# Later first Fourier steps, another order of the matmuls in a weight tile, and fewer background loads: a hybrid diffusion backbone on one core

## The chip, the core and the metric

The kernel runs as one program on one core of a Trainium2 chip. The metric is the device time in microseconds (us) from the start of the program to its end on that core. Times are medians of several runs; the profile comes from one execution, and its figures are set against that execution's own time. The engines named here are PE (TensorE: matmuls; "PEld" is its weight load), DVE (VectorE), ACT (ScalarE), and SP (SyncE, which issues all the loads). Arrays in the on-chip memory have 128 partitions.

## The reference

Two layers over 256 tokens of width 2048, with a context of 256 tokens. The even layer has retention heads, a Fourier mixing and gates; the odd layer is a gated short convolution. Cut to what matters here:

```python
def _fourier(u, fno_w):
    b, L, _ = u.shape
    ug = u.reshape(b, L, G_B, GB_DIM).astype(jnp.float32)
    f = jnp.fft.fft2(ug, axes=(1, 3), norm='ortho').real
    y = jnp.einsum('blgc,gcd->blgd', f.astype(u.dtype), fno_w)
    return y.reshape(b, L, B_WIDTH)
...
def _even_layer(hx, hc, w_in, decay_logit, fno_w, w_out, need_ctx):
...
    yx = jnp.concatenate([_merge_heads(ret_x, hx.dtype) * jax.nn.silu(gax),
                          _fourier(ux, fno_w) * jax.nn.silu(gbx)], axis=-1) @ w_out
...
def _odd_layer(h, w_in, conv_w, w_out, rows):
    bg, cg, xt, g = jnp.split(h @ w_in, 4, axis=-1)
    y = bg * _conv3(cg * xt, conv_w, rows) * jax.nn.silu(g)
    return y @ w_out

def reference(x, c, ctx, c_ctx, ada_w, ada_b, norm_w, ev_w_in, ret_decay_logit, fno_w, ev_w_out,
              od_w_in, conv_w, od_w_out, final_norm_w):
...
    for i in range(DEPTH):
        shift_x, scale_x, gate_x = jnp.split((sc @ ada_w[i] + ada_b[i])[:, None, :], 3, axis=-1)
...
        hx = _modulate(x, norm_w[i], shift_x, scale_x)
...
        x = x + gate_x * yx
    return _rmsnorm(x, final_norm_w)
```

All of it is float32. Nearly all the work lies in the products `h @ w_in` and `y @ w_out`, some 400 MB of weights, each read once.

## The kernel before

**A product.** The activations are kept transposed, channels on partitions, and split in two: 256 columns of a rounded high part and 256 of the rest, one after the other (`split_act`, `modulate`). A weight tile is 1 MB, 128 x 2048, loaded by `load_raw` into one of three buffers `raw`. `split_w` cuts it into four pieces of 512 columns; for each, ACT casts the high part `whi` (line 94) and DVE subtracts it to get the low part `wlo` (line 59), six buffers of each. `group_t` (line 126) computes 256 output channels from two or four such tiles: a piece holds two slices of 128 input channels (`k2`), and for each slice and each half `m` of the output channels there are two matmuls, both noted at line 56. The first, called H here, multiplies 128 x 128 of `whi` with all 512 columns; the second, L, multiplies the same part of `wlo` with the first 256. So a tile is 16 pairs of H and L, and a group of two tiles 32 pairs. Sums stay in PSUM; `lr` then adds the two column halves. `group_n` (name `gN`) and `group_d` (`gD`) are variants with three matmuls a step, all of 512 or all of 256 columns.

**Work hung between.** Two lists run beside the groups. `hook()` pops one entry of `stages` after the second and the fourth piece of a tile, so four times in a group of two tiles: a *quarter*. `bg()` pops a background task at the start of a tile: it loads one row block of `adaT` (1 MB, in a `raw` buffer) and reduces it on DVE (line 378) to one column of modulation values. There are 64 tasks. With `quiet[0]` set none is taken, with `often[0]` set one at every tile, without it one at every second. `finish_mods(first, last)` runs the tasks still missing up to `last`, all at once, and then uses their values.

**The order.** (1) Context and first retention pair, until about 154 us. (2) Four pairs of retention heads, until about 527; keys go to two streams (token and context), the rest to one. Background tasks run in it up to the fourth pair's queries. (3) Fourier stage. `u0` and `u1` are the two halves of the folded Fourier input; each takes 16 steps, `step(kc)`, of six matmuls into `pu` and two into `pd`, on weights that `fold(kc)` makes ahead: a sum and a difference on DVE (`ef`, lines 65 and 68), then the same cast and subtraction as above. `step(0)` also runs `fold(0)`. These steps are hung into the groups of the Fourier gate, `gate_of(0..3)` for `u0` and `gate_of(4..7)` for `u1`, one a quarter. Steps 0, 2, 4, 6 of `u0` also fold the activations (`fold_x`). The buffers of this stage, `ef` among them, are taken from a pool that opens when the retention's pool has been closed. (4) The even layer's output projection, `project(w0o)`: eight row blocks of four tiles, of which the first, `t_out`, still carries the last Fourier pieces; `quiet` is off from there to the fifth, and set for the blocks 6 and 7. (5) The odd layer: 16 blocks, each four groups of two tiles; background tasks from its second block on, at every second tile. (6) Its projection, `project(w1o)`, again eight row blocks, and the final norm.

Each engine works through its own queue in order. The order in these queues is made when the program is built: instructions are placed by a simulated timeline, the earlier one in the program first among those that the simulation finds ready. So a matmul may stand ahead of one that is written before it.

Of the kernel before, what the change touches and what calls it, by code (L numbers as in the profile page):

```python
# [22 lines left out]
H = 8  # L23
# [12 lines left out]
def body(tc, a, out):  # L36
    nc = tc.nc
    es = ExitStack()
    with es:
# [6 lines left out]
        def psum(name):  # L46
            return pp.tile([P, 2, 512], F32, tag="ps", name=name)
# [7 lines left out]
        def mm(o, l, r, start, stop):  # L55
            nc.tensor.matmul(o, l, r, start=start, stop=stop, skip_group_check=True)  # L56
# [7 lines left out]
        def add(o, x, y):  # L64
            nc.vector.tensor_tensor(o, x, y, op=ALU.add)  # L65
# [17 lines left out]
        def load_raw(src):  # L83
            raw = wp.tile([P, 2048], F32, tag="raw", name="raw")
            nc.sync.dma_start(raw[:], src)
            return raw
# [10 lines left out]
        def split_w(raw, spare=None):  # L97

            parts = []
            for pc in range(4):  # L100
                w = tuple(t[:] for t in spare()) if spare and pc == 3 else slot()
                cut(raw[:, pc * 512:(pc + 1) * 512], *w)
                parts.append(w)
            return parts

        tasks, stages = [], []

        turn = [0]
        quiet = [False]
        often = [True]  # L110

        def bg():

            if quiet[0]:
                return
            turn[0] ^= 1
            if tasks and (turn[0] or often[0]):
                tasks.pop(0)()

        def hook():  # L120
            if stages:
                f = stages.pop(0)
                if f is not None:
                    f()

        def group_t(wd, i0, nkt, streams):

            ps = [psum("gT") for _ in streams]
            for kt in range(nkt):
                raw = load_raw(wd[i0 + kt])  # L130
                bg()
                for pc, (hi, lo) in enumerate(split_w(raw)):
                    for k2 in range(2):
                        kc = kt * 8 + pc * 2 + k2
                        fst, lst = kc == 0, kc == nkt * 8 - 1
                        for t, st in zip(ps, streams):
                            x = st[kc // 2]
                            for m in range(2):
                                c0 = k2 * 256 + m * 128
                                mm(t[:, m, :], hi[:, c0:c0 + 128], x[:, kc % 2, :], fst, False)  # L140
                                mm(t[:, m, 0:256], lo[:, c0:c0 + 128], x[:, kc % 2, 0:256], False, lst)
                    if pc % 2:
                        hook()
            return ps
# [129 lines left out]
        def gather():  # L274

            gs = rp.tile([P, 512], F32, tag="cst", name="gs")
            nc.vector.tensor_copy(gs[:], gp[:])
            return gs
# [63 lines left out]
        for e in range(8):  # L342
            w = wn
# [14 lines left out]
            if more:  # L358
                gemv(raws[3], 3)
                gs = gather()  # L360
# [115 lines left out]
        for pr in range(4):  # L476
# [23 lines left out]
            def heads():  # L500
                return [retention(hh, mk[hh], q, k, kc, lambda: vbox[0]) for hh in range(2)]

            if pr == 0:
                kc = rp.tile([P, 2, 256], F32, tag="kc", bufs=1, name="kc")
# [3 lines left out]
                h0, h1 = heads()  # L508
                stages += [None, h0[0], h1[0], h0[1], h0[2], h1[1], None, h1[2]]
                keep((pvx, pvc))  # L510
            elif pr < 3:
                k, kc = keys()
                q = queries()
                h0, h1 = heads()
# [3 lines left out]
            else:  # L518
                k, kc = keys()
# [5 lines left out]
                h0, h1 = heads()  # L525
# [8 lines left out]
            for hh, hd in enumerate((h0, h1)):  # L534
                y = yA[2 * pr + hh] = act_tile(YA[2 * pr + hh], f"yA{2 * pr + hh}")
                t = hd[3]["t"]
# [215 lines left out]
        u0, u1 = half(0), half(1)  # L752
        gs = [fourier(g, u0 if g < 4 else u1) for g in range(8)]

        def both(*fs):
            def f():
                for x in fs:
                    x()
            return f

        def folds(kc):
            def f():
                if kc % 2 == 0 and kc < 8:
                    fold_x(fp, 4 + kc // 2)
                    ends(4 + kc // 2)
            return f

        stages += [both(lambda kc=kc: u0.step(kc), folds(kc)) for kc in range(15)]
        stages += [both(lambda: u0.step(15), gs[0][0])]
        for g in range(4):  # L770
            gate_of(g)

# [3 lines left out]
        for g in range(4, 8):  # L776
# [4 lines left out]
        g4[2]()  # L781
        stages += [both(g4[3], g5[1], g6[0], g5[2]), both(g4[4], g5[3], g6[1], g7[0], g6[2]),
                   both(g5[4], g6[3], g7[1], g7[2]), both(g6[4], g7[3]), g7[4]]
        quiet[0] = False
        t_out, = group_t(a["w0o"], 0, 4, [ys])
        f_es.close()

# [11 lines left out]
        def project(wd, xs, gcol, xin, acc, first=None, post=None):  # L799


            def res(b, m, v, src):
                nc.vector.scalar_tensor_tensor(x1[b][:, m, :], v, mods[:, gcol + 2 * b + m:gcol + 2 * b + m + 1],
                                               src[:, m, :], op0=ALU.mult, op1=ALU.add)

            tot = None
            for b in range(8):
                src = xin(b)
                quiet[0] = b >= 6
                if b < 7:  # L810
                    t = first if b == 0 and first is not None else group_t(wd, 4 * b, 4, [xs])[0]
                    s = lr(l1, t)
                    for m in range(2):
                        res(b, m, s[:, m, :], src)
                    if b == 0:
                        nc.scalar.square(acc[:], x1[b][:])
                    else:
                        sq = l1.tile([P, 2, 256], F32, tag="t2", bufs=5, name="sq")
                        nc.scalar.square(sq[:], x1[b][:])
                        add(acc[:], acc[:], sq[:])  # L820
                    for m in range(2 if post is not None else 0):
                        nc.scalar.activation(x1[b][:, m, :], x1[b][:, m, :], AF.Copy,
                                             scale=cols[:, post + 2 * b + m:post + 2 * b + m + 1])
                else:
                    t = group_d(wd, 4 * b, 4, xs)
                    tot = bank("tot")
                    for m in range(2):
                        mm(tot[:, 0:256], ones[:], acc[:, m, :], m == 0, False)

                    warm = l1.tile([P, 1], F32, tag="warm", name="warm")  # L830
                    nc.scalar.activation(warm[:], acc[:, 0, 0:1], AF.Sqrt)
                    sq = l1.tile([P, 2, 256], F32, tag="t2", bufs=5, name="sq")
                    for m in range(2):
                        res(b, m, t[:, m * 256:m * 256 + 256], src)
                        nc.scalar.square(sq[:, m, :], x1[b][:, m, :])
                        mm(tot[:, 0:256], ones[:], sq[:, m, :], False, m == 1)
            return rstd_bc(l1, tot[:, 0:256], D)
# [6 lines left out]
        acc0 = l1.tile([P, 2, 256], F32, tag="acc", name="acc0")  # L844
        rs1 = project(a["w0o"], ys, 0, reload, acc0, t_out)
        finish_mods(16, 48)
        often[0] = False
        nc.vector.scalar_tensor_tensor(mods[:, 16:32], mods[:, 16:32], 1.0, cols[:, C_NW1:C_NW1 + 16],
                                       op0=ALU.add, op1=ALU.mult)

# [1 line left out]
        h1 = [act_tile(HF[e], f"h1_{e}") for e in range(8)]  # L852
# [3 lines left out]
        w1 = a["w1"]  # L856
        y1 = []
        for b in range(16):
            tcg, = group_t(w1, b * 8, 2, [h1])
            scg = lr(l1, tcg, "scg", 2)  # L860
            txt, = group_t(w1, b * 8 + 2, 2, [h1])
            z = lr(l1, txt, "z", 2)
            mul(z[:], z[:], scg[:])
            cv = l1.tile([P, 2, 256], F32, tag="cv", bufs=2, name="cv")
            for m in range(2):
                w = [cols[:, C_CV + j * 32 + 2 * b + m:C_CV + j * 32 + 2 * b + m + 1] for j in range(3)]
                z4 = z[:, m, :].rearrange("p (r w) -> p r w", w=64)
                c4 = cv[:, m, :].rearrange("p (r w) -> p r w", w=64)
                nc.vector.tensor_scalar(cv[:, m, :], z[:, m, :], w[1], None, op0=ALU.mult)
                nc.vector.scalar_tensor_tensor(c4[:, :, 1:64], z4[:, :, 0:63], w[0], c4[:, :, 1:64],  # L870
                                               op0=ALU.mult, op1=ALU.add)
                nc.vector.scalar_tensor_tensor(c4[:, :, 0:63], z4[:, :, 1:64], w[2], c4[:, :, 0:63],
                                               op0=ALU.mult, op1=ALU.add)
            tbg, = group_t(w1, b * 8 + 4, 2, [h1])
            sbg = lr(l1, tbg)
            mul(cv[:], cv[:], sbg[:])
            tg, = group_t(w1, b * 8 + 6, 2, [h1])
            sg = silu_lr(l1, tg, "t2", 5)
            mul(cv[:], cv[:], sg[:])
            y1.append(act_tile(YA[b] if b < 8 else f"hx{b - 8}", f"y1_{b}"))  # L880
            split_act(y1[b], cv[:])
            quiet[0] = False
# [123 lines left out]
```

## Time and profile before

| | |
|---|---|
| median of 3 runs | 1856.43 us (1849.19 to 1857.1) |
| profiled execution, its time | 1855.88 us |
| profiled execution, its span | 1854.1 us |
| mean granted clock of PE | 0.987 |
| read from memory | 397 MB, 215 GB/s over the span |

The profile's page lists the busy time of each engine, then the span in 40 equal slices, the load queues, the chain of work that ended last (followed back from the last instruction, at each step to what released it), and the costliest groups of instructions. A group reads: line, engine, operation, output and inputs by the program's names, shapes, count | busy time in us, mean ns of one | idle time before them and what ended it. Matmuls are pipelined, so the listed length of one is longer than the distance to the next one; distances are read from starts, or from a row of the chain with its length and count.

### The profile page before, as it was taken

The numbers are of one execution on the slowest core, as the hardware profiler recorded it, in microseconds if no ns is written. First come the engines' busy times: TensorE is split into PE (matmuls) and PEld (weight loads), VectorE is DVE, ScalarE is ACT, GpSimd is POOL, SyncE is SP. The second block draws the span as 40 slices with busy tenths as digits, with TensorE's granted clock in tenths as the row PEclk, the third lists the DMA queues.
The fourth block names the chain that finished last, engine by engine and source line by source line (L and its number), as shares of the span: only waits on it lengthen the run. The fifth ranks groups of instructions, "written<-read, shape, count | busy, mean of one in ns | idle before, by whom it ended". The sixth has DMA issues, their size and how long they took to land.

```text
span 1854.1 us, 26639 instructions
## 1 busy us (share of the span) xinstructions
PE 1795.8 (97%) x10086; PEld 1520.3 (82%) x10086; DVE 1253.9 (68%) x2001; ACT 898.7 (48%) x1493; POOL 0.2 (0%) x4
## 2 busy tenths in 40 slices
PE   5999999999979999999999999999999999999997
PEld 3667888888858888878978888888888888888886
DVE  5448858668479688779688766666666666665554
ACT  4225626354446455434555555555555555555553
POOL 0000000000000000000000000000000000000000
PEclk9999999999989999999999999999999999999999
DMA  9886555655336455789547655555555555555552
GB/s 393 341 315 270 220 211 218 245 198 219 135 120 243 170 198 210 272 329 367 223 157 274 231 192 189 182 183 187 192 188 182 183 186 193 188 182 182 190 189 99
DMA packets 58738, 400.87 MB, mean 216 GB/s; under 512 B 6512, under 2 KB 6896, under 8 KB 11376
## 3 DMA queue, kind: packets, MB, share of 16 engines
q1 hardware_dynamic: 58608, 399.16, 58.8%
q8 instruction: 79, 1.29, 0.3%
q14 instruction: 51, 0.42, 0.1%
HBM read 397.03 MB, written 2.10 MB: 215 GB/s over the span
## 4 chain that ended last, share of the span: by engine, by line
PE 91%; DVE 4%; DMA 3%; ACT 1%; issue 1%; SPq 0%; DVEq 0%; ACTq 0%
PE gT L56 67%; PE gN L56 7%; PE gD L56 2%; PE pu L56 2%; PE gemv L56 2%; PE o L56 1%; PE pvx L56 1%; PE pk L56 1%; PE pvc L56 1%; DVE wlo L59 1%; DMA raw<-w0o 1%; PE pd L56 1%; PE S L56 1%; DMA raw<-adaT 1%; PE pq L56 1%
## 5 line engine op out<-in xcount | busy, mean ns | idle before, releaser
L59 DVE TENSOR_TENSOR wlo<-raw,whi 128x512 fp32r<-128x512 f32 x1024 | 693.3, 689 | 410.1 <-ACT whi L94 391.8
L94 ACT CAST whi<-raw 128x512 fp32r<-128x512 f32 x1024 | 623.3, 620 | 714.8 <-PE gT L56 498.9
L56 PE MATMUL gT<-h,whi 128*128 128x512 f32 x2048 | 724.9, 399 | 4.2 <-DVE h L205 4.2
L56 PE MATMUL gT<-h,wlo 128*128 128x256 f32 x2048 | 575.0, 281 | 0.0
L56 PEld LDWEIGHTS gT<-h,whi 128*128 128x128 f32 x2048 | 385.3, 188 | 100.6 <-issue 4.5
L56 PEld LDWEIGHTS gT<-h,wlo 128*128 128x128 f32 x2048 | 387.6, 189 | 0.4
L56 PE MATMUL gT<-hx,whi 128*128 128x512 f32 x576 | 208.8, 401 | 1.8 <-ACT v L497 1.6
L378 DVE CUSTOM_DVE_ANT_0 raw<-raw,scb 128x2048 f32<-128x2048 f32 x64 | 146.5, 2289 | 60.4 <-DMA raw<-adaT 57.4
L56 PE MATMUL gT<-hx,wlo 128*128 128x256 f32 x576 | 162.6, 282 | 0.0
L56 PE MATMUL gT<-y,whi 128*128 128x512 f32 x448 | 158.3, 399 | 0.0
L56 PEld LDWEIGHTS gT<-hx,whi 128*128 128x128 f32 x576 | 108.3, 188 | 28.5 <-ACT v L497 2.1
L56 PE MATMUL gT<-y,wlo 128*128 128x256 f32 x448 | 125.8, 281 | 0.0
L56 PEld LDWEIGHTS gT<-hx,wlo 128*128 128x128 f32 x576 | 109.0, 189 | 2.2 <-DVE wlo L59 0.6
L56 PEld LDWEIGHTS gT<-y,whi 128*128 128x128 f32 x448 | 84.2, 188 | 21.0
L56 PEld LDWEIGHTS gT<-y,wlo 128*128 128x128 f32 x448 | 84.6, 189 | 0.0
L56 PE MATMUL gT<-yA,whi 128*128 128x512 f32 x224 | 81.5, 403 | 2.3 <-ACT whi L94 2.3
L56 PE MATMUL gT<-yB,whi 128*128 128x512 f32 x224 | 79.4, 397 | 0.6 <-ACT whi L94 0.6
L56 PE MATMUL gT<-yA,wlo 128*128 128x256 f32 x224 | 64.4, 287 | 3.6 <-DVE wlo L59 3.5
L56 PE MATMUL gT<-yB,wlo 128*128 128x256 f32 x224 | 62.9, 282 | 0.6 <-DVE wlo L59 0.5
L188 ACT COPY lr_r<-gT 128x512 f32<-128x512 f32 x103 | 59.9, 582 | 3.1 <-PE gT L56 3.1
L94 ACT CAST whi<-ef 128x512 fp32r<-128x512 f32 x64 | 39.3, 620 | 42.3 <-DVE ef L65 15.0
L56 PE MATMUL gN<-whi,hx 128*128 128x512 f32 x192 | 59.6, 392 | 0.0
(283 smaller groups left out, 2166.5 us busy)
## 6 DMA issues: line engine op xcount, KB each, us to landing
raw<-w SPq DMA_DIRECT2D x168, 1024.0 KB, 4.8
raw<-adaT SPq DMA_DIRECT2D x64, 1024.0 KB, 5.0
raw<-ada SPq DMA_DIRECT2D x32, 1024.0 KB, 7.2
raw<-w0o SPq DMA_DIRECT2D x32, 1024.0 KB, 5.2
raw<-w1o SPq DMA_DIRECT2D x32, 1024.0 KB, 4.8
raw<-w0g SPq DMA_DIRECT2D x16, 1024.0 KB, 4.8
raw<-w0u SPq DMA_DIRECT2D x16, 1024.0 KB, 4.8
raw<-w0s SPq DMA_DIRECT2D x8, 1024.0 KB, 5.6
```

The source lines that it names most:

```text
L56: nc.tensor.matmul(o, l, r, start=start, stop=stop, skip_group_check=True)
L59: nc.vector.tensor_tensor(o, x, hi.bitcast(F32), op=ALU.subtract)
L94: nc.scalar.copy(hi, x)
L188: nc.scalar.copy(r[:], t[:, :, 256:512])
L378: nc.vector.tensor_tensor_reduce(out=raw[:], in0=raw[:], in1=scb[:], scale=1.0, scalar=0.0, op0=ALU.mult, op1=ALU.add, accum_out=gv[:, j:j ...
```

## The change

It has three parts. In `group_t` the order inside a piece is spelled out: the low part goes first (`LOW`), and where two streams share a tile, both take a weight before the next weight comes. Some groups get `settle=True`: in their first tile the second and third piece go in the order `MIRRORED` and the fourth in `HIGH`. In `u0` the first step moves from the first to the fourth quarter of the gate groups, and three quarters later on take two steps. The background tasks go at every second tile from `t_out` on, instead of after the first projection; in return row block 6 of that projection has tasks, too.

```diff
@@ -123,22 +123,32 @@
                 if f is not None:
                     f()
 
-        def group_t(wd, i0, nkt, streams):
+
+        LOW = "L0 H0 L1 H1 L2 H2 L3 H3".split()
+        HIGH = "H0 L0 H1 L1 H2 L2 H3 L3".split()
+        MIRRORED = "H0 L0 L1 H1 H2 L2 L3 H3".split()
+
+        def group_t(wd, i0, nkt, streams, settle=False):
 
             ps = [psum("gT") for _ in streams]
+            last = nkt * 8 - 1
             for kt in range(nkt):
                 raw = load_raw(wd[i0 + kt])
                 bg()
                 for pc, (hi, lo) in enumerate(split_w(raw)):
-                    for k2 in range(2):
-                        kc = kt * 8 + pc * 2 + k2
-                        fst, lst = kc == 0, kc == nkt * 8 - 1
+                    todo = LOW
+                    if settle and kt == 0 and pc:
+                        todo = HIGH if pc == 3 else MIRRORED
+                    seen = set()
+                    for what, j in ((x[0], int(x[1])) for x in todo):
+                        k2, m = j // 2, j % 2
+                        kc, c0 = kt * 8 + pc * 2 + k2, j * 128
+                        n = 512 if what == "H" else 256
+                        w = (hi if what == "H" else lo)[:, c0:c0 + 128]
                         for t, st in zip(ps, streams):
-                            x = st[kc // 2]
-                            for m in range(2):
-                                c0 = k2 * 256 + m * 128
-                                mm(t[:, m, :], hi[:, c0:c0 + 128], x[:, kc % 2, :], fst, False)
-                                mm(t[:, m, 0:256], lo[:, c0:c0 + 128], x[:, kc % 2, 0:256], False, lst)
+                            mm(t[:, m, 0:n], w, st[kc // 2][:, kc % 2, 0:n], kc == 0 and j not in seen,
+                               kc == last and j in seen)
+                        seen.add(j)
                     if pc % 2:
                         hook()
             return ps
@@ -765,8 +775,15 @@
                     ends(4 + kc // 2)
             return f
 
-        stages += [both(lambda kc=kc: u0.step(kc), folds(kc)) for kc in range(15)]
-        stages += [both(lambda: u0.step(15), gs[0][0])]
+        def steps(*kcs):
+            def f():
+                for kc in kcs:
+                    u0.step(kc)
+                    folds(kc)()
+            return f
+
+        stages += [None, None, None, steps(0), steps(1), steps(2), steps(3, 4), steps(5), steps(6), steps(7, 8), steps(9),
+                   steps(10), steps(11, 12), steps(13), steps(14), both(steps(15), gs[0][0])]
         for g in range(4):
             gate_of(g)
 
@@ -781,7 +798,7 @@
         g4[2]()
         stages += [both(g4[3], g5[1], g6[0], g5[2]), both(g4[4], g5[3], g6[1], g7[0], g6[2]),
                    both(g5[4], g6[3], g7[1], g7[2]), both(g6[4], g7[3]), g7[4]]
-        quiet[0] = False
+        quiet[0] = often[0] = False
         t_out, = group_t(a["w0o"], 0, 4, [ys])
         f_es.close()
 
@@ -806,9 +823,9 @@
             tot = None
             for b in range(8):
                 src = xin(b)
-                quiet[0] = b >= 6
+                quiet[0] = b >= 7 - (post is not None)
                 if b < 7:
-                    t = first if b == 0 and first is not None else group_t(wd, 4 * b, 4, [xs])[0]
+                    t = first if b == 0 and first is not None else group_t(wd, 4 * b, 4, [xs], b in (1, 3))[0]
                     s = lr(l1, t)
                     for m in range(2):
                         res(b, m, s[:, m, :], src)
@@ -844,7 +861,6 @@
         acc0 = l1.tile([P, 2, 256], F32, tag="acc", name="acc0")
         rs1 = project(a["w0o"], ys, 0, reload, acc0, t_out)
         finish_mods(16, 48)
-        often[0] = False
         nc.vector.scalar_tensor_tensor(mods[:, 16:32], mods[:, 16:32], 1.0, cols[:, C_NW1:C_NW1 + 16],
                                        op0=ALU.add, op1=ALU.mult)
 
@@ -856,7 +872,8 @@
         w1 = a["w1"]
         y1 = []
         for b in range(16):
-            tcg, = group_t(w1, b * 8, 2, [h1])
+            settle = b in (1, 2, 8)
+            tcg, = group_t(w1, b * 8, 2, [h1], settle)
             scg = lr(l1, tcg, "scg", 2)
             txt, = group_t(w1, b * 8 + 2, 2, [h1])
             z = lr(l1, txt, "z", 2)
@@ -871,7 +888,7 @@
                                                op0=ALU.mult, op1=ALU.add)
                 nc.vector.scalar_tensor_tensor(c4[:, :, 0:63], z4[:, :, 1:64], w[2], c4[:, :, 0:63],
                                                op0=ALU.mult, op1=ALU.add)
-            tbg, = group_t(w1, b * 8 + 4, 2, [h1])
+            tbg, = group_t(w1, b * 8 + 4, 2, [h1], b < 2)
             sbg = lr(l1, tbg)
             mul(cv[:], cv[:], sbg[:])
             tg, = group_t(w1, b * 8 + 6, 2, [h1])
```

## Prediction

> **What bounds the kernel now.** I read the page first: the span, the busy shares, the clock and the chain of work that ended last.
>
> ```profile
> span 1854.1 us, 26639 instructions
> PE 1795.8 (97%) x10086; PEld 1520.3 (82%) x10086; DVE 1253.9 (68%) x2001; ACT 898.7 (48%) x1493; POOL 0.2 (0%) x4
> PEclk9999999999989999999999999999999999999999
> PE 91%; DVE 4%; DMA 3%; ACT 1%; issue 1%; SPq 0%; DVEq 0%; ACTq 0%
> ```
>
> The kernel is bound by its matmuls: 91% of the chain is PE. So there are two ways to gain: fill the few holes, or make the same matmuls follow each other faster. For the second I read the chain in order of time, where each row gives a start, a length and a count.
>
> ```profile
> 269.94 5.64 PE gT L56 x32
> 275.58 3.45 PE o L56 x16
> 279.03 5.55 PE gT L56 x32
> 285.01 5.65 PE gT L56 x32
> 290.66 3.45 PE o L56 x16
> 294.12 5.55 PE gT L56 x32
> 300.10 33.92 PE gT L56 x192
> ...
> 433.86 43.58 PE gN L56 x192
> ...
> 933.54 883.76 PE gT L56 x4992
> 1817.31 23.05 PE gD L56 x192
> ```
>
> A tile of `group_t` is 16 pairs: H, the high weight part over 512 columns, and L, the low part over 256. The same 16 pairs take 5.55 us in two rows (346.9 ns a pair) and 5.64 to 5.65 in three others (353 ns); 192 matmuls take 33.92 (353.3). There are **two paces**, and a stretch keeps the one that it starts in: it is short after `o`, long after the short norm matmuls that follow the second row. The sizes alone would give the short one: in unbroken runs a 512-column matmul takes 43.58/192 = 227 ns and a 256-column one 23.05/192 = 120 ns, together 347. The odd layer and most of its projection are one stretch of 2496 pairs at 883.76/2496 = 354.1 ns, the long pace to the end (the half-speed start and a few waits make up the last 0.8).
>
> For the holes I read the waits and the windows (length, then busy time and instructions of PE, PEld, DVE, ACT, POOL; clock; DMA share; GB/s).
>
> ```profile
> ACT whi L94 <- DMA raw<-w0o: 54.7, 16, 6.2
> ...
> 500.00:526.00 26.00, 26.00 (x141) 22.88 (x141) 12.09 (x18) 11.18 (x17) 0.00 (x0) 1.00 0.31 118
> 526.00:535.00 9.00, 1.90 (x11) 1.33 (x9) 4.93 (x13) 4.31 (x6) 0.00 (x0) 0.76 0.00 0
> 535.00:550.00 15.00, 11.35 (x25) 6.10 (x26) 14.94 (x42) 8.71 (x16) 0.00 (x0) 0.61 0.42 140
> 550.00:570.00 20.00, 20.00 (x103) 16.32 (x102) 19.65 (x42) 12.56 (x21) 0.00 (x0) 0.97 0.56 211
> 570.00:590.00 20.00, 20.00 (x104) 16.01 (x103) 19.46 (x35) 11.17 (x20) 0.00 (x0) 1.00 0.69 257
> 590.00:612.00 22.00, 22.00 (x119) 18.30 (x118) 18.98 (x31) 12.51 (x21) 0.00 (x0) 1.00 0.67 245
> ...
> 796.00:864.00 68.00, 63.52 (x349) 53.14 (x348) 55.94 (x78) 25.50 (x48) 0.00 (x0) 1.00 0.93 348
> ```
>
> Two holes matter. Between 526 and 550 PE issues 36 matmuls, at most 36 x 227 ns = 8.2 us of work in 24 us, and the granted clock falls to 0.76 and 0.61: about 16 us lost. Between 796 and 864 (the output projection of the even layer) 349 matmuls need 349/2 x 346.9 = 60.5 us and take 68: 7.5 us lost, at a DMA share of 0.93.
>
> **The change, part by part.**
>
> *Fewer background rows.* Each background task is a 1 MB load, which SP issues between the weight tiles, and a pass on DVE.
>
> ```profile
> L378 DVE CUSTOM_DVE_ANT_0 raw<-raw,scb 128x2048 f32<-128x2048 f32 x64 | 146.5, 2289 | 60.4 <-DMA raw<-adaT 57.4
> raw<-adaT SPq DMA_DIRECT2D x64, 1024.0 KB, 5.0
> 1000.00:1100.00 100.00, 100.00 (x568) 86.72 (x567) 72.84 (x118) 50.66 (x84) 0.00 (x0) 1.00 0.62 225
> ```
>
> Now a task goes with every tile of the projection, so 2 MB are wanted per 5.6 us, some 375 GB/s; the starved window reached 348. After the change it is every second tile, 1.5 MB, 280 GB/s. The odd layer does exactly that after 1000 (six tasks in twelve tiles) and PE is busy for 100 of 100 us. So the wait on `raw<-w0o` should go. I take 7.0 of the 7.5 us, bounds 4 and 7.5, and 1 us (0 to 3) for the four tiles before, which carry two tasks instead of four. What could come due is the deadline: `finish_mods(16, 48)` pops whatever is missing in one burst, each task 5.0 us of landing and 2.3 of DVE. Count: 34 tasks are taken before the Fourier stage (4 + 12 + 12 + 6 tiles), then 4 + 24 tiles at every second one give 14, in all 48, just enough, since row block 6 carries tasks now, too. No burst. Sixteen tasks instead of six are left for the odd layer, under the cover that the 1000 to 1100 row shows (DVE 73 of 100); without it each would cost 2.3 us.
>
> *First steps of u later.* I read what PE waited for at 526.
>
> ```profile
> 515.22 0.62 ACT L94 CAST whi<-raw 128x512 fp32r<-128x512 f32 x1 [0.77 <-PE gT L56]
> ...
> 546.39 2.18 ACT L94 CAST whi<-raw 128x512 fp32r<-128x512 f32 x4
> ...
> 534.74 0.68 DVE L65 TENSOR_TENSOR ef<-raw 128x512 f32<-128x512 f32 x1
> 535.34 0.69 DVE L68 TENSOR_TENSOR ef<-raw 128x512 f32<-128x512 f32 x1
> 536.49 0.62 DVE L59 TENSOR_TENSOR wlo<-ef,whi 128x512 fp32r<-128x512 f32 x1
> 537.37 0.68 DVE L59 TENSOR_TENSOR wlo<-ef,whi 128x512 fp32r<-128x512 f32 x1
> ...
> L59 DVE TENSOR_TENSOR wlo<-ef,whi 128x512 fp32r<-128x512 f32 x32 | 21.0, 682 | 1.4 <-ACT whi L94 1.0 <-PE pd L56 0.4
> L59 DVE TENSOR_TENSOR wlo<-raw,whi 128x512 fp32r<-128x512 f32 x31 | 20.6, 683 | 2.4 <-ACT whi L94 2.2 <-ACT lr_r L188 0.2
> ```
>
> Step 0 of u needs the `ef` fold, whose buffer exists only once the retention pool is closed, at 534.7. Only half a gate tile stands before step 0, and PE has done that by 526. The gate splits then stop at 515.2 and go on at 546.4, behind the folds. After the change 48 more matmuls, 24 x 0.35 = 8.4 us, stand before step 0, and their operands hang on no new pool; PE runs them while it now idles. This is not all gain, because DVE is the next bound: from 535 to 612 it is busy 14.94 + 19.65 + 19.46 + 18.98 = 73.0 of 77 us. The work is the same, except that some five gate splits (the last of tile 0, four of tile 1; 20.6/31 = 0.66 us each, 3.3 us) move ahead of 535, where DVE is half idle. Then DVE is through at 535 + 69.7 = 605 at best; PE's own work (70 us between 526 and 612, less the hole's) would allow 600. I take the end at 606.5, **5.5 us** earlier; bounds 12 (PE's end) and, if the three double steps leave PE waiting for DVE at a halved clock, a loss, which is a rival below. SP issues the same loads, the `w0u` ones behind one more `w0g` tile; three buffers of `raw` cover that, and without them a load costs its 5 us once.
>
> *Low parts first, and the settle groups.* The matmuls are the same in number and size. L first waits for the slower of the two splits: where a split is late, PE loses at most one H (0.23 us) that it could have run. With the starved tiles mostly gone I take +1 us, bounds 0 and +3. With two streams the order becomes L L H H instead of L H L H, in six tiles only; with the other short stretches of the even layer, some of which have the short pace now and some the long one, I set it to 0, bounds -2.4 and +1.
>
> The large term is the pace. Does a broken alternation cost anything by itself? The build has made one by chance at the odd layer's start:
>
> ```profile
> 950.08 0.63 PE L56 MATMUL gT<-h,whi 128*128 128x512 f32 x2
> 950.54 0.28 PE L56 MATMUL gT<-h,wlo 128*128 128x256 f32 x1
> 950.66 0.39 PE L56 MATMUL gT<-h,whi 128*128 128x512 f32 x1
> 950.88 0.40 PE L56 MATMUL gT<-h,wlo 128*128 128x256 f32 x2
> 951.12 0.40 PE L56 MATMUL gT<-h,whi 128*128 128x512 f32 x1
> ```
>
> H H L H L L takes 951.12 - 950.08 = 1.04 us, three pairs at 346.7 ns. So MIRRORED, which doubles H and L in turn, should itself run at the short pace. What counts is the pace at which alternation goes on behind it. The rows after `o` show that an interruption can leave it short, the row at 933.54 that it can leave it long. The settle groups interrupt five times in the odd layer (blocks 0, 1, 1, 2, 8) and twice in each projection. One success is enough, since nothing stalls PE afterwards. From the third group of block 0 on there are 2496 - 64 = 2432 pairs; at 353.3 - 346.9 = 6.4 ns each that is **15.6 us**; and about half of the even projection, 0.6 us. Bounds: 0 (the pace stays) and 17.5 (all 2496 at 7 ns).
>
> The Trainium skill speaks against this term: its page "TensorE: Matmul & The Clock Gate", section "Back-to-back issue gap", gives the time from matmul to matmul by the number of columns alone, so that order cannot matter. The two chain rows of 5.55 and 5.65 us for the same 32 matmuls disagree with it; by it this term would be 0.
>
> Sum, against the profiled execution's 1855.9 us (span 1854.1 and 1.8 around it; the median of the runs shown is 1856.4): 1855.9 - 7.0 - 1.0 - 5.5 + 1.0 - 15.6 - 0.6 = 1827.2.
>
> **The rivals.**
>
> *The pace stays long.* The alternation behind a settle group falls back into the 353.3 ns cycle. For it: after the broken order at 950 just that happened. Against it: the rows at 279 and 294, and five tries. Then 1827.2 + 16.2 = 1843.4.
>
> *It turns only late or for part of the way*, say from block 8: 1024 + 448 pairs x 6.4 = 9.4 us of the 15.6: 1833.4.
>
> *Slower: DVE starves u, and the clock is halved.* PE will have some 57 us of work in the 71 us after 535, in small portions between folds. In the 535 to 550 row the granted clock was 0.61 with PE waiting between portions. At a mean clock of 0.5 to 0.6 over the whole stage 57 us become 95 to 114, so it ends at 630 to 649 instead of 612: some +27 in place of -5.5. With the long pace that is 1876, with the short one 1860. It decides against the change once the stage's mean clock falls below 57/77 = 0.74. Against it: 550 to 570 still had DVE at 98%, and 0.97.
>
> The same page, section "Part 1: The HAM clock gate (the "warmup" mystery)", has the clock halved after a window of about 3.4 us without activity. The 9 us hole agrees with it; portions every microsecond would then not halve it.
>
> *It does not do what it says.* The build's order by a simulated timeline may pull the folds ahead of the gate matmuls again; then the 5.5 us are missing: 1832.7. This lies in the forecast's own range.
>
> **How the numbers follow.** Forecast 0.62 (own range 1818 to 1837); the pace stays 0.17; it turns in part 0.09; the clock is halved 0.07 with the long pace and 0.03 with the short; 0.02 for gains given back otherwise (1855). The range 1817 to 1848 takes in the first three cases and the bounds of the holes. About 0.5%, 9 us, is what a measurement of this kernel can tell from no change. Faster by more: 0.62 + 0.17 + 0.09 = 0.88; within: 0.05; slower: 0.07.
>
> **What would show it.** Right: one long chain row of gT in the odd layer with count x length giving 347 ns a pair; no wait on `raw<-w0o` beyond a few us and PE busy for the whole projection; gate matmuls between 526 and 535 with a clock near 1.0, and u done near 606. Wrong: 353 ns a pair behind the settle groups; a burst of `adaT` tasks at the end of the projection; a clock under 0.8 between 535 and 606; whi or wlo as releaser of gT matmuls in the odd layer.

## The result, and the profile after

| | before | changed |
|---|---|---|
| median | 1854.03 us (4 runs, 1849.19 to 1857.1) | 1832.02 us (4 runs, 1831.2 to 1834.0) |
| ratio to before | | 0.9885, interval [0.9859, 0.9911] |
| profiled execution: time, span | 1855.88, 1854.1 us | 1831.67, 1829.8 us |

Some 21 us faster, where 28.7 were forecast. The page of the changed kernel, in its lines on the span, the engines, the clock and the chain:

```profile
span 1829.8 us, 25929 instructions
PE 1781.8 (97%) x10086; PEld 1514.5 (83%) x10086; DVE 1248.8 (68%) x2001; ACT 902.6 (49%) x1493; POOL 0.2 (0%) x4
PEclk9999999999999999999999999999999999999999
PE 94%; DVE 3%; DMA 1%; issue 1%; ACT 1%; SPq 0%; DVEq 0%
```

The chain is PE for 94% instead of 91%, its share of DMA falls from 3% to 1%: the holes are smaller. The windows of the two holes (length, busy time and count of PE, PEld, DVE, ACT, POOL; clock; DMA share; GB/s):

```profile
526.00:535.00 9.00, 8.25 (x47) 6.98 (x45) 5.03 (x7) 5.06 (x7) 0.00 (x0) 1.00 0.29 117
535.00:550.00 15.00, 11.48 (x40) 7.28 (x41) 14.78 (x43) 9.88 (x18) 0.00 (x0) 0.77 0.47 154
550.00:570.00 20.00, 17.93 (x81) 13.65 (x80) 19.84 (x45) 11.57 (x21) 0.00 (x0) 0.91 0.56 201
570.00:590.00 20.00, 19.18 (x99) 15.29 (x98) 18.76 (x36) 10.78 (x19) 0.00 (x0) 1.00 0.62 235
590.00:612.00 22.00, 22.00 (x115) 17.90 (x114) 19.84 (x33) 13.41 (x24) 0.00 (x0) 1.00 0.62 226
...
796.00:864.00 68.00, 68.00 (x394) 59.41 (x393) 51.49 (x74) 33.51 (x55) 0.00 (x0) 1.00 0.80 296
```

Between 526 and 550 PE issues 87 matmuls instead of 36, and the first window runs at the full clock. From 535 on DVE is as busy as before (14.78 + 19.84 + 18.76 + 19.84 = 73.2 us), and PE waits for the splits of the folds: from 535 to 612 5.1 us in all for casts on ACT, which themselves wait for the folds on DVE, and 2.1 us for subtractions on DVE. The last matmul of `u0` into `pu` starts at 609.9 us; before the change it was 613.1. In the even projection 394 matmuls go through in the 68 us that took 349, and ACT's wait for the `w0o` loads (54.7 us before) is gone.

In the chain the odd layer stands in one row again:

```profile
761.67 124.97 PE gT L56 x717
...
915.87 878.00 PE gT L56 x4991
1793.87 23.04 PE gD L56 x192
```

878.0 us for what took 883.8: only 5.8 us of the 15.6 forecast. Windows inside it say why. At the long pace 100 us hold 566 starts, at the short one 577; the count adds one or two matmuls that reach over an edge.

```profile
1100.00:1200.00 100.00, 100.00 (x579) 87.42 (x578) 70.49 (x110) 51.96 (x87) 0.00 (x0) 1.00 0.61 221
...
1290.00:1390.00 100.00, 100.00 (x568) 86.67 (x567) 62.47 (x101) 50.52 (x84) 0.00 (x0) 1.00 0.53 188
...
1665.00:1700.00 35.00, 35.00 (x205) 30.60 (x204) 19.43 (x30) 17.53 (x30) 0.00 (x0) 1.00 0.57 202
1710.00:1790.00 80.00, 80.00 (x455) 69.36 (x454) 44.83 (x69) 40.52 (x69) 0.00 (x0) 1.00 0.53 188
```

The pace is short around 1100, long around 1290, short around 1665, long behind 1710. It changes exactly at the settle groups. By the starts of the matmuls (kept to the ns in the trace), the third group of block 0 left the long pace behind it, the first of block 1 the short one, the third of block 1 the long one, the first of block 2 the short one (some 755 pairs of it), block 8 the long one (some 1075 pairs), row block 1 of the last projection the short and row block 3 the long one. All three settle groups that met the short pace turned it to the long one.

### The profile page after: what moved, and what is told of

Read it like the earlier page. It is cut to its first block, busy times and chain, and to the rows that moved or that the text cites. A ratio compares the mean times of both kernels' runs of the same rounds, so it can differ in the third digit from the quotient of the medians.

```text
span 1829.8 us, 25929 instructions
## 1 busy us (share of the span) xinstructions
PE 1781.8 (97%) x10086; PEld 1514.5 (83%) x10086; DVE 1248.8 (68%) x2001; ACT 902.6 (49%) x1493; POOL 0.2 (0%) x4
## 4 chain that ended last, share of the span: by engine, by line
PE 94%; DVE 3%; DMA 1%; issue 1%; ACT 1%; SPq 0%; DVEq 0%
PE gT L56 71%; PE gN L56 7%; PE gD L56 3%; PE pu L56 2%; PE gemv L56 2%; PE o L56 2%; PE pvx L56 1%; PE pk L56 1%; PE pvc L56 1%; DMA raw<-adaT 1%; PE pd L56 1%; PE S L56 1%; DVE wlo L59 1%; PE pq L56 1%; PE pP L56 1%
## 5 line engine op out<-in xcount | busy, mean ns | idle before, releaser
L56 PE MATMUL gT<-h,wlo 128*128 128x256 f32 x2048 | 568.5, 280 | 3.4 <-ACT h L214 3.4
L65 DVE TENSOR_TENSOR t<-gT,lr_r 128x512 f32<-128x512 f32 x68 | 46.9, 690 | 31.1 <-ACT lr_r L198 31.0
```

## The experiments

Times are medians; the ratio behind each, with its interval, is to the kernel before on the same chip (1851 to 1854 us).

**What a settle group does: none, and two.** The first kernel sets `settle` to `False` everywhere. The second keeps two:

```diff
-                    t = first if b == 0 and first is not None else group_t(wd, 4 * b, 4, [xs], b in (1, 3))[0]
+                    t = first if b == 0 and first is not None else group_t(wd, 4 * b, 4, [xs], b == 3 and post is None)[0]
...
-            settle = b in (1, 2, 8)
+            settle = b == 1
...
-            tbg, = group_t(w1, b * 8 + 4, 2, [h1], b < 2)
+            tbg, = group_t(w1, b * 8 + 4, 2, [h1])
```

> The changed kernel without any settle group (all tiles in the order LOW). In the changed kernel's trace every settle group that met the short pace (347 ns a pair) left the long one (353) behind it, and most that met the long pace left the short one. Theory A, a settle group only turns the pace over: without them the odd layer and its projection keep the long pace from start to end, so the 804 + 114 short pairs there and 239 in the even projection cost 6.6 ns more each: 1832 + 7.6 = 1839 to 1840. Theory B, the settle groups do nothing and the pace wanders by itself: within 2 us of 1832, short and long stretches in other places.

> The changed kernel with two settle groups alone: row block 3 of the even projection and the first group of block 1 of the odd layer, the two places behind which the changed kernel went from 353 to 347 ns a pair. Theory A (turning over): nothing turns the pace back, so the odd layer and its projection stay at 347 ns from block 1 on; the 50 + 1074 + 239 long pairs gain 6.6 ns each, 1832 - 9 = 1823. If the pace before block 1 is another than in the changed kernel, the group turns it to the long one instead: 1838. Theory B (wandering): 1832 with several stretches of both paces.

Without settle groups 1843.2 us, 0.9946 [0.9926, 0.9967]; with two 1824.8 us, 0.9843 [0.9823, 0.9862]. The row of the odd layer in the chain, of the first kernel

```profile
767.34 126.59 PE gT L56 x717
...
923.18 884.27 PE gT L56 x4991
```

(with the one of the even projection above it) and of the second:

```profile
919.07 8.11 PE gT L56 x36
927.22 859.86 PE gT L56 x4955
```

The second chain has the first 36 matmuls, which run in part at half speed, in a row of their own. In the first kernel they take 8.8 us by their starts, so the other 4955 take 875.5 us against 859.9: 353.4 and 347.1 ns a pair, for the same matmuls in the same number. So the settle groups do decide the pace, and five of them in the odd layer are worse than one. Both times lie above what theory A gave, 1839 to 1840 and 1823, by 3 and 2 us. The four runs of each kernel lie within 4 us of each other, so the 16 us between the two paces come with the kernel and not with the single execution.

**A settle group more.**

```diff
-            settle = b in (1, 2, 8)
+            settle = b in (1, 2, 5, 8)
```

> The changed kernel with one settle group more, in the first group of block 5 of the odd layer, where its pace was short. Theory A (turning over): long from block 5, short again from block 8, long from row block 1 of the last projection, short from row block 3: the places after block 8 are turned the other way round. Long pairs: 50 + 384 + 128 in place of 50 + 1074 + 239, so 1832 - 5.3 = 1827. Rival: what a settle group leaves depends on the place and not on the pace that it meets: block 8 leaves the long pace in any case, and 384 more pairs are long: 1834.5.

1835.1 us, 0.9902 [0.9881, 0.9923]: the rival's number. The windows:

```profile
1030.00:1130.00 100.00, 100.00 (x579) 87.44 (x578) 83.58 (x124) 51.22 (x85) 0.00 (x0) 1.00 0.78 284
1150.00:1250.00 100.00, 100.00 (x568) 86.81 (x567) 62.86 (x101) 50.24 (x85) 0.00 (x0) 1.00 0.54 190
1300.00:1400.00 100.00, 100.00 (x569) 86.77 (x568) 64.59 (x107) 50.19 (x84) 0.00 (x0) 1.00 0.53 183
```

Block 5 turned short to long, as the theory of turning over says; block 8 met the long pace and left it long, which that theory excludes and the rival of the place foresaw. This run does not exclude that rival. The kernel with GpSimd does, further below: there the settle group in the first group of block 1, which leaves the short pace behind it in the kernel with two settle groups, leaves the long one. A third reading is that the point in the cycle at which the long pace is met decides. It is a cycle of three pairs, 1060 ns: H is followed by L after 241, 236 and 233 ns, L by H after 120, 113 and 117. A settle group begins with a doubled H. In all traces so far those that met the long pace behind the 241 or the 233 left the short one, those behind the 236 the long one (block 8 of the last kernel among them). That gives a test without a free choice.

**The same settle group, 32 pairs later.** In the kernel with two settle groups, the second group of block 1 takes the place of the first (`txt` in place of `tcg`).

> As the kernel with two settle groups alone, but in the odd layer the second group of block 1 takes it instead of the first. In all traces so far the long pace is a cycle of three pairs, whose H are followed after 241, 236 and 233 ns; a settle group that starts behind the 241 or the 233 leaves the short pace, one that starts behind the 236 the long one. A group has 32 pairs, two more than ten cycles; the first group of block 1 was met behind 233, so the second will be met behind 236 and leaves the long pace: the odd layer keeps 353 ns a pair, 1825 + 16 = 1841. If the settle order leaves the short pace from any point of the cycle, 1825.

1840.0 us, 0.9931 [0.9916, 0.9946], and in the chain 353.4 ns a pair:

```profile
925.11 875.53 PE gT L56 x4955
```

15 us lost by moving the same order by one group. The timeline of this kernel at the end of that settle group (start, length of one or of the merged ones, count):

```profile
980.28 0.28 PE L56 MATMUL gT<-h,wlo 128*128 128x256 f32 x1
980.40 0.40 PE L56 MATMUL gT<-h,whi 128*128 128x512 f32 x1
980.63 0.40 PE L56 MATMUL gT<-h,wlo 128*128 128x256 f32 x2
```

The settle group ends with a doubled L at 980.63, and it stands behind an H followed after 236 ns (by the starts to the ns; the rows round to 10 ns). In every settle group that left the short pace that last doubled L stood behind an H of 241 ns. So its place in the cycle should be what counts, and it can be chosen: a doubled H met behind the 236, or in the short pace, is followed by pairs of 233, then 241, so that a doubled L after three pairs falls right.

**One piece with three pairs between.** All settle groups go; one piece of a tile gets an order of its own, first in the place where the settle group had just failed:

```diff
+        NUDGE = "H0 L0 H1 L1 H2 L2 L3 H3".split()
...
-                    if settle and kt == 0 and pc:
-                        todo = HIGH if pc == 3 else MIRRORED
+                    if settle and kt == 0 and pc == 1:
+                        todo = NUDGE
```

> The kernel whose settle group in the second group of block 1 left the long pace (1840.0), with that group's second piece in the order H0 L0 H1 L1 H2 L2 L3 H3 and the other pieces LOW, in the same place and in row block 3 of the even projection. If the doubled L behind the third pair turns the long pace met behind 236 to the short one: 347 ns a pair from block 1 on, 1825. If the place is what decided: 1840.

1824.6 us, 0.9846 [0.9826, 0.9865]. The timeline there:

```profile
978.69 0.62 PE L56 MATMUL gT<-h,whi 128*128 128x512 f32 x2
...
979.61 0.40 PE L56 MATMUL gT<-h,whi 128*128 128x512 f32 x1
979.85 0.40 PE L56 MATMUL gT<-h,wlo 128*128 128x256 f32 x2
...
980.45 0.39 PE L56 MATMUL gT<-h,whi 128*128 128x512 f32 x1
...
984.26 0.40 PE L56 MATMUL gT<-h,whi 128*128 128x512 f32 x1
```

The doubled H at 978.69 was met behind 236, as in the kernel before; the doubled L at 979.85 stands 241 ns behind its H, and the eleven pairs from 980.45 to 984.26 take 346 ns each. The order inside the piece decided, in a place where the settle order had failed. Then in every group of one stream (`if len(streams) == 1 and kt == 0 and pc == 1`):

> The kernel with order LOW, no settle group, but in every group with one stream the second piece of the first tile has the order H0 L0 H1 L1 H2 L2 L3 H3: one doubled H, three pairs, one doubled L. By the gaps seen so far a doubled H behind 241 or 233 of the long cycle leaves the short pace, one behind 236 leaves the long one, as does one met in the short pace; then after three pairs the next H is followed after 241 ns, and a doubled L at that point, which ended every settle group that left the short pace, leaves the short pace again. So every group should go on at 347 ns whatever it met: 1823 to 1825, with no long stretch in the odd layer behind its second group. If the doubled parts do not add up like this, part of the groups go on at 353: 1828 to 1840.

1826.6 us, 0.9859 [0.9842, 0.9876], 1.6 us above the expected range, though there is no long stretch in the odd layer behind the second group. In the chain the odd layer takes 8 us less than in the changed kernel, but the even projection (first row) takes as long as without any settle group:

```profile
762.76 126.46 PE gT L56 x717
...
918.47 869.73 PE gT L56 x4991
```

From the fourth group on, every group of the odd layer takes 347.5 ns a pair, against 346.7 where the piece is left out: it costs some 26 ns each time. There the doubled H met the long pace once, behind 236, and then always the short one; some 60 extra pieces come to about 1.6 us. In the even projection the same order fails. By the starts, the piece is met there five times in the long cycle behind the 233, and each time the long pace goes on behind it: 126.5 us against the 125.0 of the kernel with two settle groups, 1.5 us more. So this order leaves the short pace behind it when it is met behind 236, behind 241 or in the short pace, and the long one when it is met behind 233; the settle order fails behind 236 instead. The expectation that every group would go on at 347 ns whatever it met did not come true.

**The mirrored order everywhere.**

```diff
-                    todo = LOW
-                    if settle and kt == 0 and pc:
-                        todo = HIGH if pc == 3 else MIRRORED
+                    todo = MIRRORED if len(streams) == 1 else LOW
```

> The changed kernel with the order MIRRORED (H L L H, H L L H) in every tile of every group with one stream, no LOW or HIGH there. Theory A: the long pace belongs to strict alternation alone; with H and L doubled in turn every pair takes 347 ns whatever went before. Some 1775 long pairs are left in the changed kernel, 6.6 ns each: 1832 - 11.7 = 1820. Rival: the mirrored order has a long cycle of its own, as the 351 ns a pair of the broken order at the odd layer's start before the change might say; then 1832 to 1842.

1826.0 us, 0.9853 [0.983, 0.9875], between the two:

```profile
916.07 871.32 PE gT L56 x4992
```

Its groups take 348.3 ns a pair from the third on and never change: no long cycle of alternation, but 1.6 ns above the short pace.

**The three parts alone**, each put into the kernel before. First the rows:

```diff
-        quiet[0] = False
+        quiet[0] = often[0] = False
         t_out, = group_t(a["w0o"], 0, 4, [ys])
...
-                quiet[0] = b >= 6
+                quiet[0] = b >= 7 - (post is not None)
...
-        often[0] = False
```

> The kernel before with the background rows alone: every second tile from t_out on, and row block 6 of the first projection with tasks. If the loads of the rows starved the projection, its 7 us of waiting and some of those in the four tiles ahead go: 1854.4 - 8 = 1846, and the odd layer's length stays at 353 ns a pair. If the projection is starved by something else (the splits on DVE, the order of the parts), within 2 us of 1854.

1844.0 us, 0.9951 [0.9936, 0.9966], 6 to 12 us faster by the interval:

```profile
796.00:864.00 68.00, 68.00 (x395) 59.46 (x394) 52.49 (x74) 33.80 (x55) 0.00 (x0) 1.00 0.78 291
```

The starved window is full, at a DMA share of 0.78 instead of 0.93. Then the steps alone (the `steps` list of the diff, nothing else):

> The kernel before with the later first steps of u0 alone. If the hole at 526 us was the wait for step 0, PE fills it and the end of u0 comes some 4.5 us earlier, no more, because DVE is then the bound: 1850. If the later start only moves the wait, within 2 us of 1854; if PE starved behind DVE at a halved clock, later than 1854.

1834.5 us, 0.9899 [0.9882, 0.9915], 19 us faster and far off. The chain of this kernel:

```profile
933.79 859.15 PE gT L56 x4955
```

347 ns a pair: the odd layer runs at the short pace from its second group on, though no line of its code was touched. Its first pieces are where the build doubles H and L by chance, and here the last doubled part, an L at 942.87, stood behind an H of 230 ns, where before the change, at 950.88, it stood behind one of 224. That this made the pace is argued from the traces. The same 4955 matmuls take 875.5 us at the long pace, so 16 of the 19 us are not the steps'. Then `LOW` alone, no settle group (with it, in the tiles of two streams, the new order of the streams):

> The kernel before with the order LOW in every tile and no settle group. By the sum of the prediction the low part first costs up to a few tenths of a us at each starved piece and leaves the odd layer at 353 ns a pair: 1854 to 1857. Rival: the low part first was itself worth something (no chance doubling of H and L in starved stretches, another pace in the projection): 1850 or less.

1856.8 us, 1.0021 [1.0003, 1.0038], a loss of 1 to 7 us; the odd layer at 353 ns:

```profile
940.16 875.58 PE gT L56 x4955
```

The last, to price the steps with the pace held: the kernel with the nudge in two places (1824.6) and u0's steps as before the change.

> The kernel with the order H0 L0 H1 L1 H2 L2 L3 H3 in the second group of block 1 and row block 3 (1824.6), with u0's steps back where they were before the change. Its odd layer should be at 347 ns a pair again, since that order leaves the short pace from any point of the cycle, so that the time tells what the later steps are worth by themselves: the hole of 8.7 us at 527 is back, the end of u0 is some 3 us later, 1827 to 1829. If the later steps were worth all of the 19 us that they gave alone: 1840 and more.

1830.0 us, 0.9884 [0.9867, 0.9902]; the hole is back:

```profile
526.00:535.00 9.00, 2.68 (x15) 2.02 (x13) 4.93 (x13) 4.52 (x6) 0.00 (x0) 0.76 0.00 0
535.00:550.00 15.00, 9.85 (x23) 5.35 (x24) 14.75 (x43) 8.59 (x16) 0.00 (x0) 0.61 0.43 140
```

The steps are worth 5.4 us by the medians, 7 by the ratios; the 3 us that remain of the steps alone have an interval from 0 to 6 and do not speak against it. Counted from the same row of `gN` ahead of the stage, the last matmul of `u0` into `pu` starts 3.8 us earlier with the later steps. Another 1.8 us lie behind it, where the half-speed stretch near 630 lasted 10.2 us in this profile and 6.8 in the other. The order turned the pace here too; it met the long cycle behind 241 this time. That it does so from any point of the cycle, as was expected here, is contradicted by the even projection of the kernel with the piece in every group.

**Is DVE the bound of u0 now?** The kernel with two settle groups, and in `fold` the difference of every second step on GpSimd:

```diff
-                for op in (add, dif):
+                for op in (add, pdif if kc % 2 else dif):
```

> The kernel with two settle groups alone (1824.8), and the difference of every second fold of u0 and u1 taken on GpSimd instead of DVE. If DVE is what ends the stage of u0 after the change, eight operations of 0.6 us off its queue bring the end of u0 up to 4 us earlier: 1821. If it is the wait of single steps, or GpSimd is much slower at this than DVE's 0.68 us and step and fold wait for it, the same or later: 1825 to 1835.

1843.0 us, 0.9953 [0.9937, 0.997], slower than anything expected, and it does not answer the question. The group on GpSimd, and the odd layer in the chain:

```profile
L71 POOL TENSOR_TENSOR ef<-raw 128x512 f32<-128x512 f32 x16 | 29.7, 1857 | 676.2 <-PE pu L56 539.9 <-DVE wlo L59 99.7 <-issue 26.9
...
923.77 884.48 PE gT L56 x4991
```

One difference takes 1.86 us there, against 0.68 on DVE, and the last matmul of `u0` into `pu` starts at 614.6 instead of 609.7. 16 us of the 18 lost are the pace again: the settle group of block 1 met the cycle behind 236 and left it long, though only work 350 us ahead had been moved. Same group, same place, another point of the cycle: so the place alone does not decide. That DVE bounds u0 stays argued from its 73 us, not shown.

## Why the prediction was right, point by point

The time lies in the range, and the direction holds; the sizes of the first two terms hold as totals, and the largest term came out at half to two thirds of what it said. That the sum still fell into the range is owed to the range, whose bounds took in a pace that turns only in part. Two of the prediction's own signs of being wrong did appear: 353 ns a pair behind settle groups, and a clock under 0.8 between 535 and 550.

- **Fewer rows**: forecast 8.0 us, alone 9.1 (6 to 12). The count of 48 tasks held (34 before the Fourier stage, 14 up to the end of the projection), and no burst stands in front of `finish_mods`.
- **Later steps**: forecast 5.5, with the pace held 5.4 to 7. PE fills 526 to 535 as foreseen. But `u0` was to end 5.5 us earlier, at 606.5, and its last matmul moved by 3 to 4 us, to 609.9; that the total agrees so well is in part luck. The clock still falls to 0.77 between 535 and 550 and to 0.91 behind it, which the forecast had only as a rival; its mean over 535 to 612 is 0.93, far above the 0.74 that the rival needed. The second fall is this execution's: the eight other profiles with the later steps and all folds on DVE have only the first, 3.4 or 6.8 us long. That portions every microsecond would not halve the clock is not borne out: no pause of PE there is longer than 2.8 us, and the two ahead of the second fall are 1.1 and 1.0 us.
- **Low parts first**: forecast a loss of 1 us, alone 3.9 (0.6 to 7.0). The kernel without settle groups, at 1854.4 x 0.0054 = 10 us below before, agrees: 9.1 + 5.4 - 3.9 = 10.6. The sign was right; the interval is too wide to say whether the size was too small.
- **The pace**: forecast 15.6 + 0.6. In the chains of the changed kernel and of the one without settle groups it is 884.3 - 878.0 = 6.3 in the odd layer and its projection, and 1.6 in the even one (126.59 us for the same 717 matmuls against 124.97). By the medians of the same two kernels it is 11.1 us; in the two profiles most of what lies beyond these rows stands ahead of them, and it was not traced. The mechanism was right: order alone moves a pair between 353 and 347 ns. The sentence that failed is "One success is enough, since nothing stalls PE afterwards": the settle groups themselves turn the pace back. The rival "it turns only late or for part of the way" had the number, 1833.4, and not this cause. The size forecast was there to be had: between the rows of 875.5 and 859.9 us, which start at the same matmul, lie 15.7.

The terms add up to 9.1 + 5.4 - 3.9 + 7.9 = 18.5 us against 21 measured, whose interval is 16.5 to 26; the rest is not assigned.

The rule of the Trainium skill that the forecast set against this term (page "TensorE: Matmul & The Clock Gate", section "Back-to-back issue gap", whose figures give the spacing by the number of columns alone) is contradicted by these runs: the same 4955 matmuls of the odd layer take 875.5 us with the settle order in the second group of block 1 and 859.9 with it in the first.

## What to carry to other kernels

Before a stretch of equal matmuls is called bound, divide its length by its count and compare with other stretches of the same matmuls: a few per cent can lie in the pace that they keep, not in their number. Such a pace is inherited from what ran before, so an edit far ahead can seem to gain or lose what it does not own; split the profile by stage before crediting it. When an order is put in to turn such a state, look whether it also turns it back, and use it once.

The fastest kernels run were the one with the nudge in two places (1824.6 us) and the one with two settle groups (1824.8), both faster than the changed one. Neither order is safe everywhere: the nudge left the short pace behind it when it was met behind 236 (once in each of two kernels), behind 241 and in the short pace, but the long one when it was met behind 233; the settle group left the long one behind 236. Which point is met depends on the code ahead, so after an edit the trace has to be read again.

## What the runs showed of the hardware that was not expected

- An alternation of 512- and 256-column matmuls, a weight load for each, has two steady paces: 346.7 ns a pair, about the sum of 227 and 120 that unbroken runs take, and a cycle of three pairs in 1060 ns. In an undisturbed stretch neither changes: some 2450 pairs of the long one before the change, over 2300 of the short one with the settle order once.
- A single doubled matmul can turn one into the other, and the point of the cycle decides which. In the kernel with the nudge and the early steps a doubled H behind 241 is followed by the short pace within two pairs; in the same kernel with the later steps one behind 236 is followed by the long cycle again (233, then 241 ns), until the doubled L. Why the pairs keep either pace was not tried.
- The granted clock fell to half for 3.4 to 10.2 us in all 14 profiles during the 50 small matmuls of `pm` at about 625 (8 columns each, 0.11 us apart) or right behind them, with PE never idle there. Its cause was not tried.
- GpSimd takes 1.86 us, by the profile, for a 128x512 subtraction that takes DVE 0.68.
